# RMSNorm with gelu: one two-operation VectorE instruction per row, and one gelu instruction for four rows

## The chip, the cores and the metric

The kernel runs on one core of one Trainium2 chip. The metric is the device time of one execution in microseconds (us). Before the change it is 317.47 us, the median of three runs (317.44 to 317.48).

## The reference

```python
batch, seq_len, hidden = 8, 1024, 2048                     # x is float32, 67.1 MB
rms = np.sqrt(np.mean(x ** 2, axis=-1, keepdims=True) + eps)
out = gamma * x / rms
return (0.5 * out * (1 + np.tanh(np.sqrt(2 / np.pi) * (out + 0.044715 * out ** 3)))).astype(np.float32)
```

Each of the 8192 rows of 2048 numbers is divided by its root mean square, multiplied by gamma and put through gelu. All of x is read once and an output of the same size is written once, 134 MB in total.

## The kernel before

The rows are worked in 16 groups. A group is a tile of 128 partitions with 4 rows each: 4.19 MB, in six slots that are reused in turn.

```python
P = 128; ROWS = 4; SLOTS = 6; GW = 128
x3 = x.rearrange("b s d -> (b s) d").rearrange("(g p r) d -> g p r d", p=P, r=R)     # G = 16 groups
slot = [sbuf.tile([P, R, D], FP32, name=f"slot{i}") for i in range(SLOTS)]
gamma_ps = psum.tile([P, D], FP32, name="gamma_ps")    # gamma in all partitions
# ... small tiles: ssq and rstd for all groups, ms, y, z, power (filled with -0.5)
store_pieces = {G - 1: [(0, 2), (2, 2)]}
scale_pieces = {G - 1: [(0, 1), (1, 1), (2, 1), (3, 1)]}

def load(g):                                           # issued from the SP queue
    nc.sync.dma_start(out=slot[g % SLOTS], in_=x3[g])

def squares(g):                                        # ScalarE: sum of squares, row by row
    for r in range(R):
        nc.scalar.activation(out=junk, in_=slot[g % SLOTS][:, r, :], func=ACT.Square,
                             accum_out=ssq[:, g, r : r + 1])

def scale(g):                                          # VectorE: times gamma, in place
    for r, n in scale_pieces.get(g, [(0, R)]):
        rows = slot[g % SLOTS][:, r : r + n, :]
        nc.vector.tensor_tensor(out=rows, in0=rows,
            in1=gamma_ps.unsqueeze(1).to_broadcast([P, n, D]), op=ALU.mult)

# inverse_rms(g): six small GpSimd instructions, from ssq[:, g, :] to rstd[:, g, :]

def gelu_store(g):                                     # ScalarE: gelu(rstd * row), then the store
    for r, n in store_pieces.get(g, [(0, R)]):
        for q in range(r, r + n):
            row = slot[g % SLOTS][:, q, :]
            nc.scalar.activation(out=row, in_=row, func=ACT.Gelu_apprx_tanh,
                                 scale=rstd[:, g, q : q + 1])
        nc.scalar.dma_start(out=o3[g, :, r : r + n, :], in_=slot[g % SLOTS][:, r : r + n, :])

for g in range(SLOTS):
    load(g)
# ... gamma: one DMA of 16 pieces of 128 numbers, then four matmuls with ones into gamma_ps
for g in range(G + 1):
    if g < G:
        squares(g); inverse_rms(g); scale(g)
    if g:
        gelu_store(g - 1)
        if g - 1 + SLOTS < G:
            load(g - 1 + SLOTS)
```

ScalarE works in the order: squares of group g+1, gelu of group g, store of group g. A load into a slot waits until the store of what was in it has landed.

Of the kernel before, what the change touches and what calls it, by code (L numbers as in the profile page):

```python
# [1 line left out]

# [4 lines left out]

FP32 = mybir.dt.float32
ALU = mybir.AluOpType
ACT = mybir.ActivationFunctionType  # L10

P = 128
ROWS = 4
SLOTS = 6

GW = 128


@with_exitstack
def kernel(  # L20
    ctx: ExitStack,
    tc: tile.TileContext,
    x: bass.AP,
    gamma: bass.AP,
    eps: bass.AP,
    out: bass.AP,
):




    nc = tc.nc
    D = x.shape[-1]
    R = ROWS
    eps_f = float(eps)
    x3 = x.rearrange("b s d -> (b s) d").rearrange("(g p r) d -> g p r d", p=P, r=R)
    o3 = out.rearrange("b s d -> (b s) d").rearrange("(g p r) d -> g p r d", p=P, r=R)
    G = x3.shape[0]

    sbuf = ctx.enter_context(tc.tile_pool(name="sbuf", bufs=1))  # L40
    psum = ctx.enter_context(
        tc.tile_pool(name="psum", bufs=1, space=bass.MemoryType.PSUM)
    )
    slot = [sbuf.tile([P, R, D], FP32, name=f"slot{i}") for i in range(SLOTS)]
    gamma_row = sbuf.tile([1, D // GW, GW + 16], FP32, name="gamma_row")
    ones = sbuf.tile([1, P], FP32, name="ones")
    warm = sbuf.tile([1, 1], FP32, name="warm")
    power = sbuf.tile([P, R], FP32, name="power")
    ssq = sbuf.tile([P, G, R], FP32, name="ssq")
    rstd = sbuf.tile([P, G, R], FP32, name="rstd")  # L50
    ms = sbuf.tile([P, R], FP32, name="ms")
    y = sbuf.tile([P, R], FP32, name="y")
    z = sbuf.tile([P, R], FP32, name="z")
    gamma_ps = psum.tile([P, D], FP32, name="gamma_ps")
    junk = psum.tile([P, D], FP32, name="junk")

    store_pieces = {G - 1: [(0, 2), (2, 2)]}
    scale_pieces = {G - 1: [(0, 1), (1, 1), (2, 1), (3, 1)]}

    def load(g):  # L60
        nc.sync.dma_start(out=slot[g % SLOTS], in_=x3[g])  # L61

    def squares(g):
        for r in range(R):
            nc.scalar.activation(  # L65
                out=junk,
                in_=slot[g % SLOTS][:, r, :],
                func=ACT.Square,
                accum_out=ssq[:, g, r : r + 1],
            )  # L70

    def scale(g):
        for r, n in scale_pieces.get(g, [(0, R)]):
            rows = slot[g % SLOTS][:, r : r + n, :]
            nc.vector.tensor_tensor(  # L75
                out=rows,
                in0=rows,
                in1=gamma_ps.unsqueeze(1).to_broadcast([P, n, D]),
                op=ALU.mult,
            )  # L80

    def inverse_rms(g):

        v = nc.gpsimd
        v.tensor_scalar(  # L85
            out=ms, in0=ssq[:, g, :], scalar1=1.0 / D, scalar2=eps_f,
            op0=ALU.mult, op1=ALU.add,
        )
        v.tensor_tensor(out=y, in0=ms, in1=power, op=ALU.pow)  # L89
        v.tensor_tensor(out=z, in0=y, in1=y, op=ALU.mult)  # L90
        v.tensor_tensor(out=z, in0=z, in1=ms, op=ALU.mult)  # L91
        v.tensor_scalar(  # L92
            out=z, in0=z, scalar1=-0.5, scalar2=1.5, op0=ALU.mult, op1=ALU.add
        )
        v.tensor_tensor(out=rstd[:, g, :], in0=z, in1=y, op=ALU.mult)  # L95

    def gelu_store(g):
        for r, n in store_pieces.get(g, [(0, R)]):
            for q in range(r, r + n):
                row = slot[g % SLOTS][:, q, :]  # L100
                nc.scalar.activation(  # L101
                    out=row, in_=row, func=ACT.Gelu_apprx_tanh,
                    scale=rstd[:, g, q : q + 1],
                )
            nc.scalar.dma_start(  # L105
                out=o3[g, :, r : r + n, :], in_=slot[g % SLOTS][:, r : r + n, :]
            )

    with tc.manual_schedule():
        for g in range(SLOTS):  # L110
            load(g)
        nc.scalar.dma_start(
            out=gamma_row[:, :, 0:GW],
            in_=gamma.rearrange("(o a b) -> o a b", o=1, b=GW),
        )
        nc.gpsimd.memset(power, -0.5)  # L116
        nc.vector.memset(warm, 0.0)  # L117
        nc.vector.memset(ones, 1.0)  # L118
        nc.scalar.activation(out=warm, in_=warm, func=ACT.Gelu_apprx_tanh)  # L119
        for k in range(0, D, 512):  # L120
            nc.tensor.matmul(  # L121
                out=gamma_ps[:, k : k + 512],
                lhsT=ones,
                rhs=gamma_row[:, k // GW : (k + 512) // GW, 0:GW],
                start=True,
                stop=True,
            )
        for g in range(G + 1):
            if g < G:
                squares(g)  # L130
                inverse_rms(g)
                scale(g)
# [6 lines that stand above are left out]
# [1 line left out]
_INS = ['x', 'gamma', 'eps']  # L140
_OUTS = [((8, 1024, 2048), 'float32')]

_NUMBERS = {'eps': 9.999999747378752e-06}


# [26 lines left out]
```

## Time and profile before

| what | before | read from |
|---|---|---|
| span of the profiled run | 316.9 us | head of the page |
| mean rate of the DMA | 424 GB/s | DMA row |
| rate from 140 to 240 us, share of the DMA engines | 433 GB/s, 1.00 | table by stage |
| VectorE, ScalarE busy | 44%, 79% | part 1 |
| one load, from issue to landing | 37.1 us | DMA issues |

The page of the profile, of the kernel before. In the rows "DMA" and "GB/s" each digit or number is one of 40 equal slices of the span. The lines with q1 and q10 are the two DMA queues, loads (q1) and stores (q10): number of packets, megabytes, and the time that the packets took as a share of 16 DMA engines' span.

```profile
span 316.9 us, 473 instructions
PE 7.2 (2%) x8; PEld 2.5 (1%) x8; DVE 139.4 (44%) x21; ACT 251.1 (79%) x194; POOL 32.3 (10%) x101
...
DMA  8999999999999999999999999999999999999995
GB/s 328 414 451 426 434 393 459 401 459 402 459 405 455 426 434 431 430 434 426 438 426 455 410 455 418 443 426 430 434 430 435 422 459 405 459 414 447 422 420 230
...
q1 hardware_dynamic: 2304, 67.11, 49.5%
q10 hardware_dynamic: 2480, 67.12, 49.1%
```

The DMA engines are in the top tenth in every slice but the ends. The two queues share them about equally. A share times the span is a time per engine: loads 0.495 × 316.9 = 156.9 us, stores 0.491 × 316.9 = 155.6 us.

The table by stage, kernel before, from 140 to 240 us. After the engines' busy times come the granted TensorE clock, the DMA share and GB/s.

```profile
140.00:240.00 100.00, 0.00 (x0) 0.00 (x0) 43.44 (x5) 81.06 (x63) 9.98 (x30) 1.00 1.00 433
```

The groups by form, kernel before: busy time and mean duration of one, then the idle time before them and what ended it.

```profile
L75 DVE TENSOR_TENSOR slot<-slot,gamma_ps 128x8192 f32<-128x8192 f32 x15 | 130.3, 8688 | 142.4 <-ACT junk L65 142.4
L101 ACT ACTIVATE slot<-slot,rstd 128x2048 f32<-128x2048 f32 x64 | 122.8, 1989 | 0.9 <-ACT slot L101 0.9
L65 ACT ACTIVATE junk<-slot 128x2048 f32<-128x2048 f32 x64 | 120.4, 1881 | 47.3 <-DMA slot<-in_x_dram 43.7 <-ACT slot L101 2.1
```

ScalarE waits 43.7 us in total for loads and almost not at all for VectorE. The timeline of the kernel before shows the first gelus, the first store, and the squares that start two later groups and the last one (start, duration, in us):

```profile
30.93 7.67 ACT L101 ACTIVATE slot<-slot,rstd 128x2048 f32<-128x2048 f32 x4
38.62 0.36 ACTq L105 DMA_DIRECT2D out_dram<-slot  x1
...
140.10 1.88 ACT L65 ACTIVATE junk<-slot 128x2048 f32<-128x2048 f32 x1 [3.67 <-DMA slot<-in_x_dram]
...
236.84 1.88 ACT L65 ACTIVATE junk<-slot 128x2048 f32<-128x2048 f32 x1 [3.69 <-DMA slot<-in_x_dram]
...
276.24 1.88 ACT L65 ACTIVATE junk<-slot 128x2048 f32<-128x2048 f32 x1 [3.66 <-DMA slot<-in_x_dram]
```

Five groups lie between the lines at 140.10 and 236.84 us, so one group takes (236.84 − 140.10) / 5 = 19.35 us.

### The profile page before, as it was taken

How to read it: one execution, taken by the hardware profiler on the slowest of the kernel's cores; microseconds unless marked ns; L12 is line 12 of the kernel's file. 1: busy time of each engine (PE TensorE's matmuls, PEld its weight loads, DVE VectorE, ACT ScalarE, POOL GpSimd, SP SyncE). 2: the span in 40 equal slices, each digit the busy share in tenths (PEclk: the TensorE clock that was granted, in tenths of full speed). 3: DMA queues.
4: the chain of work that ended last, by engine and by line, in shares of the span. 5: the costliest groups of instructions: out<-in, count | busy, mean ns of one | idle time of the engine just before them, and what ended most of it. 6: DMA issues, size and time to landing. Idle time of an engine off the chain costs nothing.

```text
span 316.9 us, 473 instructions
## 1 busy us (share of the span) xinstructions
PE 7.2 (2%) x8; PEld 2.5 (1%) x8; DVE 139.4 (44%) x21; ACT 251.1 (79%) x194; POOL 32.3 (10%) x101
## 2 busy tenths in 40 slices
PE   0900000000000000000000000000000000000000
PEld 0300000000000000000000000000000000000000
DVE  0038909090919191732808246091550905582000
ACT  1379999999999997959689595995959859599800
POOL 0020102020202020202002020020200102001000
DMA  8999999999999999999999999999999999999995
GB/s 328 414 451 426 434 393 459 401 459 402 459 405 455 426 434 431 430 434 426 438 426 455 410 455 418 443 426 430 434 430 435 422 459 405 459 414 447 422 420 230
DMA packets 4787, 134.25 MB, mean 424 GB/s; under 512 B 544, under 2 KB 560, under 8 KB 560
## 3 DMA queue, kind: packets, MB, share of 16 engines
q1 hardware_dynamic: 2304, 67.11, 49.5%
q10 hardware_dynamic: 2480, 67.12, 49.1%
q14 instruction: 3, 0.02, 0.0%
HBM read 67.12 MB, written 67.11 MB: 424 GB/s over the span
## 4 chain that ended last, share of the span: by engine, by line
DMA 56%; ACT 33%; issue 5%; ACTq 1%; SPq 0%
DMA slot<-in_x_dram 30%; DMA out_dram<-slot 26%; ACT slot L101 19%; ACT junk L65 14%; ACTq L105 1%; SPq L61 0%; ACTq L101 0%; ACTq L65 0%
## 5 line engine op out<-in xcount | busy, mean ns | idle before, releaser
L75 DVE TENSOR_TENSOR slot<-slot,gamma_ps 128x8192 f32<-128x8192 f32 (+1 forms) x19 | 139.2, 7340 | 147.0 <-ACT junk L65 147.0
L65 ACT ACTIVATE junk<-slot 128x2048 f32<-128x2048 f32 x64 | 120.4, 1881 | 47.3 <-DMA slot<-in_x_dram 43.7
L101 ACT ACTIVATE slot<-slot,rstd 128x2048 f32<-128x2048 f32 x64 | 122.8, 1989 | 0.9 <-ACT slot L101 0.9
L85 POOL TENSOR_SCALAR ms<-ssq 128x4 f32<-128x4 f32 x16 | 3.1, 194 | 247.5 <-ACT junk L65 247.5
L89 POOL TENSOR_TENSOR y<-ms,power 128x4 f32<-128x4 f32 x16 | 16.1, 1009 | 1.3
L65 ACT ACTIVATION_READ_ACCUMULATOR junk<-slot 128x1 f32 x64 | 12.0, 188 | 0.0
L121 PE MATMUL gamma_ps<-gamma_row,ones 1*128 1x512 f32 x8 | 7.2, 1072 | 8.4 <-DMA gamma_row<-in_gamma_dram 8.4
L95 POOL TENSOR_TENSOR rstd<-z,y 128x4 f32<-128x4 f32 x16 | 3.2, 201 | 1.3
L91 POOL TENSOR_TENSOR z<-z,ms 128x4 f32<-128x4 f32 x16 | 3.2, 201 | 1.3
L90 POOL TENSOR_TENSOR z<-y 128x4 f32<-128x4 f32 x16 | 3.2, 199 | 1.3
L92 POOL TENSOR_SCALAR z<-z 128x4 f32<-128x4 f32 x16 | 3.1, 194 | 1.4
L121 PEld LDWEIGHTS gamma_ps<-gamma_row,ones 1*128 1x128 f32 x8 | 2.5, 325 | 11.5 <-issue 11.5
L119 ACT ACT_TABLE_LOAD x1 | 1.3, 1283 | 1.3 <-PEq L153 1.3
L117 DVE MEMSET warm<- 1x1 f32 x1 | 0.1, 59 | 0.8 <-PEq L153 0.8
L119 ACT ACTIVATE warm<-warm 1x1 f32<-1x1 f32 x1 | 0.2, 202 | 0.0
L118 DVE MEMSET ones<- 1x128 f32 x1 | 0.2, 165 | 0.0
L116 POOL MEMSET power<- 128x4 f32 x1 | 0.1, 102 | 0.3 <-POOLq L153 0.3
L153 POOL MEMSET const-float32-0.0<- 128x1 f32 x1 | 0.1, 99 | 0.2 <-issue 0.2
L153 POOL MEMSET const-bfloat16-1.0<- 128x1 bf16 x1 | 0.1, 102 | 0.0
L153 POOL MEMSET const-uint8-127<- 128x1 uint8 x1 | 0.1, 102 | 0.0
L153 POOL MEMSET const-float32-1.0<- 128x1 f32 x1 | 0.1, 99 | 0.0
## 6 DMA issues: line engine op xcount, KB each, us to landing
slot<-in_x_dram SPq DMA_DIRECT2D x16, 4096.0 KB, 37.1
out_dram<-slot ACTq DMA_DIRECT2D x15, 4096.0 KB, 38.6
out_dram<-slot ACTq DMA_DIRECT2D x2, 2048.0 KB, 15.0
gamma_row<-in_gamma_dram ACTq DMA_DIRECT2D x1, 8.0 KB, 7.5
```

Of the source, the lines that this page charges most:

```text
L65: nc.scalar.activation(out=junk, in_=slot[g % SLOTS][:, r, :], func=ACT.Square, accum_out=ssq[:, g, r : r + 1],)
L75: nc.vector.tensor_tensor(out=rows, in0=rows, in1=gamma_ps.unsqueeze(1).to_broadcast([P, n, D]), op=ALU.mult,)
L85: v.tensor_scalar(out=ms, in0=ssq[:, g, :], scalar1=1.0 / D, scalar2=eps_f, op0=ALU.mult, op1=ALU.add,)
L89: v.tensor_tensor(out=y, in0=ms, in1=power, op=ALU.pow)
L90: v.tensor_tensor(out=z, in0=y, in1=y, op=ALU.mult)
L91: v.tensor_tensor(out=z, in0=z, in1=ms, op=ALU.mult)
L92: v.tensor_scalar(out=z, in0=z, scalar1=-0.5, scalar2=1.5, op0=ALU.mult, op1=ALU.add)
L95: v.tensor_tensor(out=rstd[:, g, :], in0=z, in1=y, op=ALU.mult)
L101: nc.scalar.activation(out=row, in_=row, func=ACT.Gelu_apprx_tanh, scale=rstd[:, g, q : q + 1],)
L105: nc.scalar.dma_start(out=o3[g, :, r : r + n, :], in_=slot[g % SLOTS][:, r : r + n, :])
L119: nc.scalar.activation(out=warm, in_=warm, func=ACT.Gelu_apprx_tanh)
L121: nc.tensor.matmul(out=gamma_ps[:, k : k + 512], lhsT=ones, rhs=gamma_row[:, k // GW : (k + 512) // GW, 0:GW], start=True, stop=True,)
```

## The change

Since gelu applies 1/rms as a scale per partition, it needs one instruction per row. If VectorE multiplies by 1/rms and gamma at once, gelu needs no scale and can take four rows in one instruction. That saves ScalarE the fixed part of three instructions per group. Gamma's load is cut into 2 pieces instead of 16.

```diff
-GW = 128
+GW = 1024
-    scale_pieces = {G - 1: [(0, 1), (1, 1), (2, 1), (3, 1)]}
 def scale(g):
-        for r, n in scale_pieces.get(g, [(0, R)]):
-            rows = slot[g % SLOTS][:, r : r + n, :]
-            nc.vector.tensor_tensor(out=rows, in0=rows,
-                in1=gamma_ps.unsqueeze(1).to_broadcast([P, n, D]), op=ALU.mult)
+        for r in range(R):
+            row = slot[g % SLOTS][:, r, :]
+            nc.vector.scalar_tensor_tensor(
+                out=row, in0=row, scalar=rstd[:, g, r : r + 1], in1=gamma_ps,
+                op0=ALU.mult, op1=ALU.mult)
 def gelu_store(g):
-            for q in range(r, r + n):
-                row = slot[g % SLOTS][:, q, :]
-                nc.scalar.activation(out=row, in_=row, func=ACT.Gelu_apprx_tanh,
-                    scale=rstd[:, g, q : q + 1])
+            rows = slot[g % SLOTS][:, r : r + n, :]
+            nc.scalar.activation(out=rows, in_=rows, func=ACT.Gelu_apprx_tanh)
 # ... the matmul's slice of gamma_row follows GW
```

More of the change, by code (lines that the diff above doesn't have):

```diff
@@ L72, in scale @@
     def scale(g):
-        for r, n in scale_pieces.get(g, [(0, R)]):
-            rows = slot[g % SLOTS][:, r : r + n, :]
-            nc.vector.tensor_tensor(
-                out=rows,
-                in0=rows,
-                in1=gamma_ps.unsqueeze(1).to_broadcast([P, n, D]),
-                op=ALU.mult,
+        for r in range(R):
+            row = slot[g % SLOTS][:, r, :]
+            nc.vector.scalar_tensor_tensor(
+                out=row, in0=row, scalar=rstd[:, g, r : r + 1], in1=gamma_ps,
+                op0=ALU.mult, op1=ALU.mult,
             )
@@ L98, in gelu_store @@
         for r, n in store_pieces.get(g, [(0, R)]):
-            for q in range(r, r + n):
-                row = slot[g % SLOTS][:, q, :]
-                nc.scalar.activation(
-                    out=row, in_=row, func=ACT.Gelu_apprx_tanh,
-                    scale=rstd[:, g, q : q + 1],
-                )
+            rows = slot[g % SLOTS][:, r : r + n, :]
+            nc.scalar.activation(out=rows, in_=rows, func=ACT.Gelu_apprx_tanh)
             nc.scalar.dma_start(
-                out=o3[g, :, r : r + n, :], in_=slot[g % SLOTS][:, r : r + n, :]
+                out=o3[g, :, r : r + n, :], in_=rows
             )
@@ L123 @@
                 lhsT=ones,
-                rhs=gamma_row[:, k // GW : (k + 512) // GW, 0:GW],
+                rhs=gamma_row[:, k // GW, k % GW : k % GW + 512],
                 start=True,
```

## The prediction

> **What bounds it now.** The DMA engines. The table by stage shows a DMA share of 0.94 to 1.03 from 8 us to 312 us, at 406 to 442 GB/s (steady stretches 431 to 434). 134.25 MB at 433 GB/s is 310 us of the 316.9 us span; the rest is start-up (0 to 8 us at 329 GB/s) and about 3 us after the last bytes. The Trainium skill, "DMA: Bandwidth & Descriptors", § Specifications, gives a fabric ceiling of 435 GB/s; the trace agrees: 433 is all there is. The engines have slack: VectorE 44%, ScalarE 79%. From 120 us on, the timeline has one group of four rows every 19.34 us (8.39 MB at 434 GB/s), and ScalarE idles 3.66 us in each, waiting for a load.
>
> **Removed, added, moved, per group.**
> - ScalarE: four gelus take 7.58 us in the chain of waits. One instruction of 8192 elements saves three fixed parts. Estimate: 2048 elements at 1.2 GHz (the skill's "ScalarE: Activation LUTs", § Specifications) are 1.71 us of the 1.895 us cadence, so 0.19 us fixed, 0.56 us saved: about 7.0 us. ScalarE's busy total falls by 8 to 12 us from 251 us.
> - VectorE: one multiply of 8192 (8.69 us) becomes four of 2048. The last group's 2048 pieces took 2.28 us each; I take the same for the two-operation form: 9.1 us, total 146 us against 139.
> - New wait: scaling now needs rstd. POOL's chain after the squares takes about 2.5 us (265.04 to 267.5 in the timeline). Scaling ends about 11.7 us after its squares instead of 8.8. In between ScalarE has the previous gelu (7.0), a store issue (0.4) and the next squares (8.15), 15.6 us, so gelu never waits for it, except in the first group (about 2 us) and perhaps the last.
> - Gamma: 8 KB in 2 pieces instead of 16. It may land a few us later or sooner, but is used at about 23 us (it lands at 8.4 now, plus 7.2 of matmuls).
>
> **On the critical path:** none of it, while transfers stay queued. Tail: the last load lands at 276.2 us; from 292 us to the end of traffic near 313.5 us some 9.2 MB flow, of which stores 14 and 15 are 8.4. So only about 0.8 MB (2 us) was queued when store 14 was issued: the tightest point. Store 14 should come 0.5 us earlier, at 291.5, the two halves of store 15 at about 295.5 and 299.6 (296.3 and 300.6 now). The last half has slack: traffic ahead of it lasts until about 308 us. At the start the first store goes out at about 40 instead of 38.6 us, but loads keep DMA busy until about 60 us.
>
> **Predicted:** 317.2 us, range 315.8 to 318.8. Faster by over 2%: 0.01; within 2%: 0.97; slower by over 2%: 0.02.
>
> **Shown right by:** DMA share about 1.00 in every stage, at 433 GB/s; group period 19.3 us; ScalarE's wait for loads up from 3.66 to about 4.2 us per group; gelu about 7.0 us; VectorE released by POOL's rstd, with 2.28 us per row; no large wait of gelu on VectorE.
>
> **Shown wrong by:** holes in the DMA row; gelu waiting on VectorE each group; rows of 4 us or more on VectorE (17 us per group still fit in 19.3, but the last store would come at about 308 us and open the tail); a transfer rate other than 433 GB/s at full share, because reads and writes overlap differently or two DMA engines carry gamma and lag; store 14 later than about 294 us.

## The result, and the profile after

The changed kernel takes 322.32 us (median of 4 runs, 321.72 to 323.49) against 317.46 us for the kernel before (4 runs). The ratio is 1.0159 (95% interval 1.0129 to 1.0189). Here and below, a ratio is the mean time of one kernel's runs over that of the other's runs of the same rounds, so it is not quite the ratio of the medians quoted. Executions over 1.5% slower than the fastest of the same kernel are left out of the means. The kernel became about 1.6% slower: still within 2%, as the prediction said, but outside its range of 315.8 to 318.8 us, and well clear of the noise.

The page of the changed kernel:

```profile
span 320.6 us, 487 instructions
PE 7.2 (2%) x8; PEld 2.5 (1%) x8; DVE 146.2 (46%) x66; ACT 240.8 (75%) x147; POOL 32.2 (10%) x101
...
DMA  8999999999999999999999999999999999999995
GB/s 328 437 413 458 413 380 442 446 409 450 405 434 413 442 418 421 425 446 405 455 397 446 401 450 409 442 405 437 409 454 397 454 397 446 425 433 437 421 427 227
...
q1 hardware_dynamic: 2304, 67.11, 50.0%
q10 hardware_dynamic: 2452, 67.12, 48.6%
```

There are no holes in the DMA row. The same 2304 packets of the load queue took longer: 0.500 × 320.6 = 160.3 us per engine, 3.4 us more than before. The stores took 0.486 × 320.6 = 155.8 us, as before. The span grew by 3.7 us. (The medians differ by 4.9 us: the profiled run of the kernel before took 318.66 us, 1.2 us above its median, so the two profiles show less than the whole loss.) So the loss that the profiles show lies in the loads' packets, at full use of the DMA engines.

The table by stage, changed kernel, the same stretch:

```profile
140.00:240.00 100.00, 0.00 (x0) 0.00 (x0) 45.66 (x21) 74.64 (x45) 9.98 (x30) 1.00 1.01 426
```

The groups by form, changed kernel:

```profile
L74 DVE SCALAR_TENSOR_TENSOR slot<-slot,rstd,gamma_ps 128x2048 f32<-128x2048 f32 x64 | 146.0, 2342 | 152.4 <-POOL rstd L92 152.4
L64 ACT ACTIVATE junk<-slot 128x2048 f32<-128x2048 f32 x64 | 120.4, 1881 | 57.3 <-DMA slot<-in_x_dram 53.6 <-ACT slot L97 2.1
L97 ACT ACTIVATE slot<-slot 128x8192 f32<-128x8192 f32 x15 | 105.2, 7014 | 1.9 <-DVE slot L74 1.9
...
L97 ACT ACTIVATE slot<-slot 128x4096 f32<-128x4096 f32 x2 | 7.2, 3616 | 1.1 <-DVE slot L74 1.1
```

The compute engines do what was predicted. Gelu takes 7.01 us for four rows, and these long gelus wait for VectorE once, 1.9 us in the first group. (The last line is the last group, which is worked in two halves.) ScalarE now waits 53.6 us for loads instead of 43.7.

The timeline, changed kernel, at the same places:

```profile
32.83 7.03 ACT L97 ACTIVATE slot<-slot 128x8192 f32<-128x8192 f32 x1 [1.93 <-DVE slot L74]
...
39.89 0.36 ACTq L98 DMA_DIRECT2D out_dram<-slot  x1
...
140.59 1.88 ACT L64 ACTIVATE junk<-slot 128x2048 f32<-128x2048 f32 x1 [5.18 <-DMA slot<-in_x_dram]
...
240.12 1.88 ACT L64 ACTIVATE junk<-slot 128x2048 f32<-128x2048 f32 x1 [4.77 <-DMA slot<-in_x_dram]
...
279.62 1.88 ACT L64 ACTIVATE junk<-slot 128x2048 f32<-128x2048 f32 x1 [4.80 <-DMA slot<-in_x_dram]
```

A group takes (240.12 − 140.59) / 5 = 19.91 us instead of 19.35. The squares of the last group start at 276.24 us before and at 279.62 us after, and from there to the end it is 40.7 and 41.0 us. So nearly all of the time is lost before the last load lands. The tail has at most 0.3 us of it.

### One level deeper: the records of single packets

The trace also has a record for each DMA packet: queue, start, duration, size. The loads and stores consist of packets of 32768 bytes (16384 in the two half stores of the last group), 128 to a transfer, 8 on each of the 16 engines. Loads and stores are counted from 0. The normal packet takes 1213 ns. The records do not name the engine; I put them to engines by joining each packet to the one that ended as it began, so single assignments can be wrong. This is one engine in each of three kernels (the third is experiment b_d12 below). "L8" is the eighth load packet of a transfer, "S8" the eighth store packet, a star is the 4-byte record that ends a transfer, and a number in brackets is a duration in ns other than 1213.

```
before   136.68L8  137.89S8  139.10L* 139.10S*  139.11L1  140.32S1  141.53L2  142.74S2  143.95L3
changed  136.62L8  137.83S7  139.03L* 139.04S8  140.25L1  141.46S*  141.47L2(1222)  142.69S1  143.89L3(1575)  145.47S2
b_d12    136.53L*  136.54S7  137.75L1  138.96S8  140.17L2  141.38S*  141.38L3  142.59S1  143.80L4
```

An engine takes one packet of each queue in turn. This fits what the Trainium skill says ("DMA: Bandwidth & Descriptors", § Queues, rings and completion order): each engine goes round robin between its queues, packet by packet. That the records of the trace are the packets of that page is taken here, not shown. Since loads and stores are equally large and both queues hold work, the offset between the end of a load and the end of a store stays what it was at the start. In the kernel before, a load and a store end at the same place (L8 S8 L* S* L1 S1) on nearly all engines. In the changed kernel the store ends one packet later on most engines and two on some, and the load packets right after that are slow on most engines.

Summed over the 16 engines and averaged over loads 6 to 15, this is the time beyond 1213 ns of the load packets, by their place in the load (us):

```
kernel     store 0 issued   1st   2nd   3rd   4th   5th   6th   7th   8th    sum
before           38.62     0.02  0.13  0.03  0.01  0.00  0.00  0.00  0.00   0.19
changed          39.89     0.00  1.65  3.10  0.36  0.06  0.03  0.00  0.08   5.28
```

The sums don't depend on how packets are put to engines; the split over the places does. (Another joining gave 1.72, 2.69 and 0.55 for the 2nd to 4th place of the changed kernel.) Over loads 4 to 15 the extra time is 69.2 us in the changed kernel and 11.6 us before; divided by 16 engines that is 4.3 and 0.7 us. The difference, 3.6 us, accounts for the 3.7 us of the span.

### The profile page after: what moved, and what is told of

Read it like the earlier page. It is cut to its first block, busy times and chain, and to the rows that moved or that the text cites. A ratio compares the mean times of both kernels' runs of the same rounds, so it can differ in the third digit from the quotient of the medians.

```text
span 320.6 us, 487 instructions
## 1 busy us (share of the span) xinstructions
PE 7.2 (2%) x8; PEld 2.5 (1%) x8; DVE 146.2 (46%) x66; ACT 240.8 (75%) x147; POOL 32.2 (10%) x101
## 3 DMA queue, kind: packets, MB, share of 16 engines
q1 hardware_dynamic: 2304, 67.11, 50.0%
## 4 chain that ended last, share of the span: by engine, by line
DMA 63%; ACT 22%; DVE 4%; issue 3%; DVEq 1%; POOL 1%; ACTq 0%; POOLq 0%; SPq 0%
DMA slot<-in_x_dram 38%; DMA out_dram<-slot 25%; ACT junk L64 12%; ACT slot L97 10%; DVE slot L74 4%; DVEq L160 1%; POOL y L86 1%; ACTq L98 0%; POOL z L88 0%; POOL z L87 0%; POOL ms L82 0%; POOL z L89 0%; POOLq L160 0%; POOL rstd L92 0%; SPq L60 0%
## 5 line engine op out<-in xcount | busy, mean ns | idle before, releaser
L74 DVE SCALAR_TENSOR_TENSOR slot<-slot,rstd,gamma_ps 128x2048 f32<-128x2048 f32 x64 | 146.0, 2342 | 152.4 <-POOL rstd L92 152.4
L64 ACT ACTIVATE junk<-slot 128x2048 f32<-128x2048 f32 x64 | 120.4, 1881 | 57.3 <-DMA slot<-in_x_dram 53.6
L97 ACT ACTIVATE slot<-slot 128x8192 f32<-128x8192 f32 (+1 forms) x17 | 112.4, 6614 | 3.1 <-DVE slot L74 3.1
```

Source lines behind the costliest of these rows:

```text
L74: nc.vector.scalar_tensor_tensor(out=row, in0=row, scalar=rstd[:, g, r : r + 1], in1=gamma_ps, op0=ALU.mult, op1=ALU.mult,)
L97: nc.scalar.activation(out=rows, in_=rows, func=ACT.Gelu_apprx_tanh)
```

## The experiments

The theory that I tested is called PHASE. Store 0 is issued 1.27 us later in the changed kernel, because the first gelu has to wait for GpSimd and VectorE. It enters the running stream of loads one packet later, and this offset stays for the whole run. (By the packet records, its first packet follows 33 load packets on 15 of the 16 engines in the kernel before; in the changed kernel it follows 34 on 13 engines and 35 on three.) At that offset the reads around the boundary are slow. The rivals are VECTOR (the two-operation instruction, or the long gelu, disturbs the DMA in SBUF) and GAMMA (gamma on two DMA engines puts the 16 engines out of step). Each experiment ran 4 times beside the kernel before, on the same chip, and all runs are fast but one of b_d3. Names with a_ start from the changed kernel, with b_ from the kernel before. All results were correct except where said.

### a_first_rows: group 0 alone with gelu row by row

```diff
-            nc.scalar.activation(out=rows, in_=rows, func=ACT.Gelu_apprx_tanh)
+            for q, m in ([(i, 1) for i in range(R)] if g == 0 else [(r, n)]):
+                part = slot[g % SLOTS][:, q : q + m, :]
+                nc.scalar.activation(out=part, in_=part, func=ACT.Gelu_apprx_tanh)
```

> The changed kernel, but group 0 alone gets four gelus of one row, so that the first can start when the first row is scaled and store 0 is issued at about 38.7 us as before, not 39.9. Everything else of the change stays. Theory PHASE (the first store entering one load packet later shifts the two DMA queues against each other by one packet for the rest of the run, and reads at the shifted boundary are slow): 317 to 318 us, the second and third packet of a load no longer slow. Theory VECTOR (the two-operation vector instruction or the long gelu takes SBUF bandwidth from the DMA) and theory GAMMA (gamma on two DMA engines puts the engines out of step): 321.5 to 323.5 us as after.

Measured: 317.52 us (317.12 to 318.76), ratio 1.0006 (0.9973 to 1.0039). All of the loss is gone, while the vector instruction in all groups, the long gelu in 15 of 16 and gamma's two pieces are still there. From the timeline and the page of a_first_rows:

```profile
38.02 0.36 ACTq L100 DMA_DIRECT2D out_dram<-slot  x1
```

```profile
span 316.1 us, 490 instructions
...
q1 hardware_dynamic: 2304, 67.11, 49.7%
```

The store goes out at 38.02 us, somewhat earlier than expected, and the load packets take 0.497 × 316.1 = 157.1 us again. This refutes VECTOR and GAMMA as causes by themselves.

### a_gamma16: gamma back in 16 pieces

```diff
-GW = 1024
+GW = 128
-                rhs=gamma_row[:, k // GW, k % GW : k % GW + 512],
+                rhs=gamma_row[:, k // GW : (k + 512) // GW, 0:GW],
```

> The changed kernel with gamma back in 16 pieces, nothing else. GAMMA: 317 to 318 us. PHASE (store 0 is still issued at about 39.9 us) and VECTOR: 321.5 to 323.5 us.

Measured: 322.53 us (321.76 to 323.0), ratio 1.0156 (1.0134 to 1.0179). Gamma's two pieces have no part in it. Store 0 was issued at 40.07 us.

### b_late1 and b_late2: a first attempt to delay store 0, which missed its dose

```diff
+            if g == 1:                       # twice in b_late2
+                nc.scalar.activation(out=junk[:, 0:1300], in_=gamma_ps[:, 0:1300], func=ACT.Square)
             if g:
                 gelu_store(g - 1)
```

> The kernel before with one extra ScalarE instruction of about 1.25 us ahead of the gelus of group 0 only, so store 0 is issued at about 39.9 us. Results stay right. PHASE: 321 to 323 us, with the second and third packet of each load slow, though nothing of the change is in it. VECTOR and GAMMA: 317 to 318 us, as ScalarE has 3.66 us of slack per group.

> As the run before with the extra instruction twice, store 0 at about 41.2 us. PHASE: the shift becomes two packets; it says the time is not that of before (318.5 us or more) but not whether it is more or less than with one. VECTOR and GAMMA: 317 to 318 us.

Measured: 318.6 us (318.0 to 319.6), ratio 1.0038 (1.0013 to 1.0063), and 317.98 us (317.6 to 318.81), ratio 1.0019 (0.9996 to 1.0042). The timeline of b_late1 shows why the number missed:

```profile
39.64 1.24 ACT L134 ACTIVATE junk<-gamma_ps 128x1300 f32<-128x1300 f32 x1 [8.81 <-DVE slot L75]
40.79 7.66 ACT L101 ACTIVATE slot<-slot,rstd 128x2048 f32<-128x2048 f32 x4
48.48 0.35 ACTq L105 DMA_DIRECT2D out_dram<-slot  x1
```

The extra instruction waited 8.81 us for VectorE, so store 0 came 9.9 us late instead of 1.25. (VectorE reads gamma_ps too; that this is the reason was not tested alone.) The intended test was not made. Still, it tells something: by the packet records the store now ends four or five packets after the load, and loads 7 to 15 have next to no slow packets. So the wide form of PHASE (any offset is slow) looked wrong, and a narrow form (one packet late is slow) was left.

### b_d3, b_d6, b_d12, b_d18: the delay in doses

Tiny instructions that touch only two 128x4 tiles wait for nothing:

```diff
+    pad = sbuf.tile([P, R], FP32, name="pad")
+            if g == 1:
+                for _ in range(6):           # 3, 6, 12 or 18
+                    nc.scalar.activation(out=pad, in_=power, func=ACT.Square)
             if g:
                 gelu_store(g - 1)
```

> The delay again, this time without touching gamma or the big tiles (the instruction of the last attempt waited about 9 us for VectorE, so that store 0 came 10 us late and not 1.25): the kernel before with six tiny ScalarE instructions ahead of the gelus of group 0, store 0 issued about 1.2 us later, at 39.7 to 40.0 us. PHASE: 321 to 323 us, the second to fourth packet of every load slow, each store's last packet coming after the next load's first one. Any theory that needs a part of the change (VECTOR, a longer gelu, gamma): 317 to 318 us.

Measured: 322.24 us (322.12 to 322.5), ratio 1.0141 (1.0109 to 1.0174). The kernel before, with 1.38 us of idle work in one place and store 0 issued 1.14 us later, is as slow as the changed one, though nothing of the change is in it. From the timeline and the page of b_d6:

```profile
30.79 1.38 ACT L136 ACTIVATE pad<-power 128x4 f32<-128x4 f32 x6
...
39.76 0.36 ACTq L106 DMA_DIRECT2D out_dram<-slot  x1
```

```profile
span 320.3 us, 479 instructions
...
q1 hardware_dynamic: 2304, 67.11, 50.3%
```

The load packets take 0.503 × 320.3 = 161.1 us.

> Twelve, store 0 about 2.4 us later, at about 41 us, so the shift is two packets. PHASE in its narrow form (only the boundary one packet late is slow, as the runs 10 us late suggest): 317 to 319 us. PHASE in its wide form (any shift is slow): 321 us or more. Other theories: 317 to 318 us.

Measured: 317.34 us (317.22 to 317.45), ratio 0.9986 (0.9948 to 1.0024). Twice the delay costs nothing. From the timeline and the page of b_d12:

```profile
41.17 0.36 ACTq L106 DMA_DIRECT2D out_dram<-slot  x1
```

```profile
span 315.6 us, 485 instructions
...
q1 hardware_dynamic: 2304, 67.11, 49.7%
```

The load packets take 0.497 × 315.6 = 156.9 us. The engine shown above from this run has the same kinds of packets beside each other as the changed kernel, only one pair later, and no slow one. The order of the packets on one engine alone doesn't decide, then. By the joined records of loads 5 to 14, 31 of the 160 load ends in the changed kernel have the store's end two packets later, and the load packets after them are slow too (0.35 us a load on that engine, against 0.32 us where it is one packet); in a_d12 below all 160 are two packets late, and none is slow (0.002 us).

> The kernel before with eighteen tiny instructions, store 0 about 3.6 us late, at about 42.3 us, so the store boundary falls three packets after the load boundary. PHASE in its narrow form: 317 to 318 us, no slow packets after group 6. If any shift but the two-packet one is slow: 321 us or more.

Measured: 317.39 us (317.22 to 317.52), ratio 0.9978 (0.9938 to 1.0018), store 0 at 42.57 us. By the joined records the store ends three packets late on 4 engines and four on 12, and the load packets are not slow. The narrow form holds here too.

> Three tiny instructions, store 0 about 0.6 us later, at about 39.2 us. PHASE has the load queue advance one packet per 1.21 us, so this lies at the edge: some engines shifted by a packet and some not, and a time between 317.3 and 322 us, by the share of shifted engines. Other theories: 317 to 318 us.

Measured: 318.76, 319.72, 323.14 and 330.12 us, ratio 1.0087 (1.0012 to 1.0162). The profiled run is the one at 330.12 us and slow, so I take nothing from its packets. As expected for the edge, this is the least steady kernel of all. That the share of shifted engines makes the spread is not shown.

### a_d12: the changed kernel made still later

The edit is that of b_d12, on the changed kernel.

> The changed kernel, made still later: twelve tiny instructions, of which the first 1.9 us only fill the wait for VectorE, so store 0 goes out about 0.5 us later than in the changed kernel, at about 40.4 us, or later if they do not overlap with that wait. PHASE: not settled, between 317.3 and 322 us, and the share of engines with a boundary one packet late should say which. Others: 321.5 to 323.5 us.

Measured: 318.34 us (317.58 to 318.82), ratio 1.0015 (0.998 to 1.005). From the timeline and the page of a_d12:

```profile
40.77 0.36 ACTq L99 DMA_DIRECT2D out_dram<-slot  x1
```

```profile
span 315.8 us, 499 instructions
...
q1 hardware_dynamic: 2304, 67.11, 49.7%
```

More work on ScalarE makes the changed kernel faster, since it moves the boundary past the bad place. The packet records agree: 0.08 us of extra time per load instead of 5.28.

### b_d6_little: do the slow packets need the compute engines?

```diff
+    def W(g):
+        return D if g < 6 else 8
     # squares, scale and gelu then work on [..., 0:W(g)]
```

> Wrong results on purpose. The kernel before with store 0 about 1.2 us late (which measured 322.24 us), but from group 6 on ScalarE and VectorE work on 8 columns of each row alone, so they hardly touch the memory. If the slow load packets are a matter of the DMA traffic alone: second and third packet of the loads still slow where the boundary stays one packet late (mean extra time of a load from 3 to 6 us over the 16 engines), 320 to 323 us. If they need the engines' accesses beside them: no slow packets from about load 8 on, 317 to 318.5 us. The boundary may move here because the queues fill differently; then the run tells nothing.

Measured: 322.86 us (322.34 to 323.3), ratio 1.015 (1.0107 to 1.0192); the result is wrong. The table by stage of b_d6_little:

```profile
140.00:240.00 100.00, 0.00 (x0) 0.00 (x0) 0.94 (x5) 9.86 (x60) 9.98 (x30) 1.00 1.00 427
```

VectorE and ScalarE work 0.94 and 9.86 us in these 100 us, not 43 and 81, and the rate is still 427 GB/s. The second and third packets again hold most of the extra time (about 4.1 of 4.38 us). So the slow packets don't need the work of ScalarE and VectorE on the tiles beside them; the DMA traffic is enough.

### a_order: does it depend on the distance between reads and writes?

```diff
+    def at(g):
+        return g // 2 + G // 2 * (g % 2)
-        nc.sync.dma_start(out=slot[g % SLOTS], in_=x3[g])
+        nc.sync.dma_start(out=slot[g % SLOTS], in_=x3[at(g)])
-                out=o3[g, :, r : r + n, :], in_=rows
+                out=o3[at(g), :, r : r + n, :], in_=rows
```

> The changed kernel, with the groups taken in the order 0, 8, 1, 9, 2, 10 and so on, so that the distance in memory between the group being loaded and the one being stored alternates between -5 and +10 groups instead of always being +5. The first store goes out at the same time, about 39.9 us. If the slow packets come from that fixed distance (reads and writes that meet in the same part of the memory): no slow packets, or slow ones in every second load only, 317 to 320 us. If from the order of the boundaries in the queues: as the changed kernel, 321.5 to 323.5 us.

Measured: 323.11 us (321.67 to 323.78), ratio 1.0143 (1.0089 to 1.0197). So the loss doesn't need the fixed distance between the group that is read and the one that is written. The place within the 4.19 MB of a group is unchanged by this edit, so a dependence on that is not excluded.

### All together

Sorted by the issue of store 0. "Extra" is the time of the load packets beyond 1213 ns, per load, summed over the engines, mean of loads 6 to 15, from the one profiled run of each kernel:

| kernel | store 0 issued (us) | median (us) | extra per load (us) |
|---|---|---|---|
| a_first_rows | 38.02 | 317.52 | 0.10 |
| before | 38.62 | 317.46 | 0.19 |
| b_d3 | 39.13 | 318.76 to 330.12 | (slow run) |
| b_d6 | 39.76 | 322.24 | 6.04 |
| changed | 39.89 | 322.32 | 5.28 |
| b_d6_little | 39.98 | 322.86 | 4.38 |
| a_order | 39.99 | 323.11 | 3.44 |
| a_gamma16 | 40.07 | 322.53 | 4.93 |
| a_d12 | 40.77 | 318.34 | 0.08 |
| b_d12 | 41.17 | 317.34 | 0.05 |
| b_d18 | 42.57 | 317.39 | 0.05 |
| b_late1 | 48.48 | 318.6 | 1.24, nearly all in load 6 |
| b_late2 | 49.87 | 317.98 | 0.92, nearly all in load 6 |

The issue of store 0 orders the runs: slow from 39.76 to 40.07 us, and not slow at 38.62 us and before, nor from 40.77 us on, whichever kernel it is; b_d3, at 39.13 us, scatters between. The two b_late kernels, whose first store comes 10 us late, come close to the kernel before again (0.4% slower; the 0.2% of b_late2 is not clear of the noise). The times of the later stores don't explain the loss: from store 3 on the changed kernel issues earlier than the kernel before (86.22 against 86.93 us) and is slow all the same. By the joined records, store 0 follows 34 load packets on most engines (10 to 14 of the 16) in each slow kernel, 32 or 33 in a_first_rows and the kernel before, and 35 to 37 in a_d12, b_d12 and b_d18. Among the slow ones, the extra time of the load packets doesn't order the medians (a_order has the least and is the slowest). Part of a_order's loss lies outside the packets: in its profiled run the DMA engines lay idle 3.3 us each on average between the first and the last packet, against 1.2 us in the changed kernel. Why, I can't say. No version beats both kernels: the best medians, of b_d12 and b_d18, are those of the kernel before. They are steadier, though: their 8 runs took 317.22 to 317.52 us, while 5 of the 21 runs of the kernel before beside the experiments took 318.3 to 319.5 us.

## Why the prediction was wrong

**Right: what bounds the kernel.** The DMA share stayed at 0.99 to 1.03 from 8 us until the last store was issued, and no engine took over.

**Right: the costs of the instructions.** Gelu of four rows: about 7.0 us predicted, 7.01 measured. ScalarE's total fell by 10.3 us (8 to 12 predicted). VectorE's total is 146.0 us (146 predicted). The estimate of gelu used the 1.2 GHz of the Trainium skill ("ScalarE: Activation LUTs", § Specifications); the measured step from 4096 to 8192 elements of the same form, 7014 − 3616 = 3398 ns for 4096 elements, agrees: 1.21 elements per ns.

**Right: the waits of gelu on VectorE.** About 2 us in the first group were predicted and 1.93 measured; none in the groups between; 1.1 us in the last group.

**Wrong: "On the critical path: none of it, while transfers stay queued".** Transfers did stay queued. The step that failed is "At the start the first store goes out at about 40 instead of 38.6 us, but loads keep DMA busy until about 60 us". The time was right (39.89), but being busy was taken to mean that nothing is lost. The prediction took 433 GB/s as fixed at full share; it was 426 in the changed kernel, with the loads' packets taking 3.4 us more. A delay of 1.27 us in one place cost 4.9 us in the medians: the first store's place among the load packets, which the prediction left out, sets how fast the load packets run later.

**Wrong in size: the period and what follows from it.** 19.3 us per group was predicted, and 19.91 us measured. The last load therefore landed 3.4 us later, and store 14 was issued at 294.67 us instead of 291.5 (later than about 294 us was on its list of what would show it wrong). ScalarE's wait for a load is about 5 us, not 4.2, since the period is longer.

**Partly foreseen:** the list of what would make the prediction wrong has "a transfer rate other than 433 GB/s at full share, because reads and writes overlap differently". The rate did differ, and the delays show that it follows the way in which loads and stores interleave. The other reason given beside it, two engines that carry gamma, is refuted by a_gamma16.

**Open:** why it is slow when most engines have an offset of one packet (in the changed kernel the others, at two, are slow as well), and not when most have none (the kernel before), two (b_d12, a_d12) or four (b_d18). The runs show that it needs neither the work of ScalarE and VectorE nor one distance between groups. A dependence on the place within a group was not tested. What happens in the memory or in the DMA engines at that boundary, no run here shows.

## What to carry to other kernels

When a kernel is bound by DMA with two saturated queues of equal transfers, the start of the first store can fix how the queues are interleaved for the rest of the run, and the rate at full use can differ between starts that are 1.2 us apart (here 433 GB/s against 425 to 427). So before a small loss is blamed on a changed instruction, delay the first store of the old kernel by a few doses: if the loss comes and goes, it belongs to the timing and not to the change. A share of 1.00 in the DMA row is not proof of a constant rate; multiply each queue's share by the span and compare the time that the same packets took.

## What the Trainium skill lacked or had wrong

- "DMA: Bandwidth & Descriptors", § Where 436 GB/s comes from, says that the HBM limit of about 358 GB/s binds transfers between HBM and SBUF. Here such transfers, loads and stores together, run at 433 GB/s from 140 to 240 us, close to the 435 that the page gives for the fabric. The sentence misleads only when read alone: the same page, § Measured, calls its own numbers single-core and keeps about 358 for both cores of a pair streaming, and this kernel runs on one core.
- The same page, § Queues, rings and completion order, has the round robin between queues, which these traces show, but not that the offset between two queues' transfers changes the rate. From 140 to 240 us it is 433 or 434 GB/s in the kernels that are not slow (before, a_first_rows, b_d12, a_d12) against 425 to 429 in the slow ones, and a packet of loads 6 to 15 takes 1254 ns on average in the changed kernel, against 1214.5 in the kernel before.
- The same page, § Why a DMA increments its semaphore by 16 and not by 1, has a rule by which a DMA whose outer dimension is 2 runs on 2 engines, and states that the issuing sequencer then does the other increments itself. The traces agree with the rule so far that gamma's load is 2 packets of 4096 bytes in the changed kernel and 16 of 512 before. The page gives no cost of that for this chip. Here the issue of gamma's load took 0.60 us in 16 pieces (0.60 in a_gamma16 too) and 1.18 us in 2, and gamma's first matmul started at 8.39 us (8.47 in a_gamma16) and 8.15 us: it made no difference that counts.
